# Hybrid decoder trunk on one core: the mixer's dense projections as numbered steps on TensorE, the small matmuls in runs between them

## Chip, cores and metric

One core of one Trainium2 chip. The metric is the device time of one execution in microseconds (us). The kernel computes in fp32; weights and activations of the large products are split into a rounded part (hi, type fp32r) and a remainder (lo), and the large products are hi·hi + hi·lo + lo·hi.

## The reference

The input x is 256 tokens x 2048. Each of two layers computes

```
h = rms_norm(x, mix_norm_w[l])
x = x + hybrid_mixer(h, w_in[l], ..., w_out[l])
h = rms_norm(x, ffn_norm_w[l])
x = x + (silu(h @ w_gate[l]) * (h @ w_up[l])) @ w_down[l]
```

and a last norm follows. `hybrid_mixer` takes one projection `h @ w_in` (7192 columns) apart into three groups of heads of 128: four mLSTM heads (mq, mk, mv, output gate mo), eight heads of forgetting attention, FoX (fq, fk, fv), and four gated DeltaNet heads (gq, gk, gv, output gate gz); 24 columns are gates. mLSTM and FoX are masked attention-like products over the 256 tokens with a decay from the gates; DeltaNet needs a triangular solve in chunks of 128. The heads' outputs are normed, gated, joined to y (256 x 2048) and multiplied by `w_out`.

## The kernel before

**Tiling.** Tokens are two tiles of 128. Weights come in units of at most 128 x 1024 (512 KB) through one DMA queue (SP's) into three buffers `raw`. For each unit ScalarE (ACT) rounds it to `whi` (L123) and VectorE (DVE) subtracts to get `wlo` (L124); both have four buffers, so unit n+4 can be rounded only when the matmuls that read unit n are done.

**Dense products.** `block_a` (L149 to 161) gives a transposed result, with the weights stationary: for a pair of 128-column outputs four units, first 32 matmuls of 512 columns on `whi` (L157), then 32 of 256 columns on `wlo` (L161). FoX's fq and fk, mLSTM's mq and mk, and DeltaNet's gkq and gvp are such pairs. `evac_a` (L163 to 170) empties one output of a pair: an ACT copy (L165), a DVE addition (L166), a DVE product (L168 or L170). `block_b` (L172 to 186) has the activations stationary and takes each unit's matmuls in threes (L184, L185, L186); mv, mog, mo, gz, fv and the output projection wo are of this kind. Their sums stand in four PSUM buffers (pool `pd`).

**Small products.** Everything between projections goes through the pool `pm`: two tags, `m` and `mg`, of two buffers each. `y_out` (L319 to 330) transposes one head's output with two matmuls against the identity (L323); an ACT and a DVE instruction (`split`, L205 and L206) empty it as hi and lo, the form in which wo wants it. The DeltaNet chain runs from the norms of q and k through the triangular solve (tiles lx, lt, lx2, lu2) and the state (y, s1p, o, ks, qs) to its last two scalings (L661, L662) and its transposes. FoX for one head is the scores fs, the maximum, two exponentials on ACT, three transposes fpt, a copy, and fo; after four heads come the sums' reciprocal, a power on POOL (L211) and a scaling of 128 x 1024 (L764), then the transposes.

**Order.** The kernel is written stage by stage: mv, mog, gates, mo, four pairs gkq, two pairs gvp, DeltaNet, gz, mLSTM heads, FoX in two groups of four heads, wo, then the feed-forward part. The framework's scheduler goes through the program with a model of the engines and may move an instruction ahead of others written earlier whenever its inputs are ready in the model; so a small product, written as one piece, ends up scattered in the dense matmuls that follow it. What comes out is one fixed queue for each engine, and each engine takes its queue strictly in order. Semaphores hold an instruction until the results that it reads are there, or until the buffer that it writes is free.

Of the kernel before, what the change touches and what calls it, by code (L numbers as in the profile page):

```python
# [12 lines left out]
F32 = mybir.dt.float32  # L13
F32R = mybir.dt.float32r
# [6 lines left out]
P = 128  # L21
# [38 lines left out]
def tile_trunk(ctx: ExitStack, tc: tile.TileContext, x: bass.AP, wu: bass.AP, prm: bass.AP,  # L60
               cst: bass.AP, fnw: bass.AP, out: bass.AP, depth: int, units: list):
    nc = tc.nc
    act, dve, pe, pool = nc.scalar, nc.vector, nc.tensor, nc.gpsimd
# [9 lines left out]
    pm = ctx.enter_context(tc.tile_pool(name="pm", bufs=2, space=bass.MemoryType.PSUM))  # L73
# [20 lines left out]
    def mps(name, tag="m"):  # L94
        return pm.tile([P, 512], F32, tag=tag, name=name)
# [235 lines left out]

    def mixer(l, norm, nxt):
        hs = norm.hs
        ys = [None] * KT

# [19 lines left out]


# [3 lines left out]
        pst = [dps("mog") for t in range(2)]  # L360
        block_b(l, "mog", 0, pst, hs, 0, KT, True, True, S + 24)
# [17 lines left out]
        ps = mps("gT")  # L379
        for t in range(2):  # L380
            pe.transpose(ps[:, t * P:(t + 1) * P], gtk[:, t], ident)
        act.copy(out=z, in_=ps[:, :S])
        gb = pr[:, l, R_GB:R_GB + 1]
        sgn = pr[:, l, R_SGN:R_SGN + 1]
        gcol = small("gcol", [3], 1)
        dve.tensor_scalar(out=gcol[:, 0:1], in0=gb, scalar1=1.0 / CAP, scalar2=None, op0=MUL)
        dve.tensor_tensor(out=gcol[:, 1:2], in0=gb, in1=sgn, op=MUL)
        dve.memset(gcol[0:32, 2:3], -1.0)
        act.activation(out=gcol[32:36, 2:3], in_=pr[32:36, l, R_AL:R_AL + 1], func=AF.Exp)
        dve.tensor_scalar(out=gcol[32:36, 2:3], in0=gcol[32:36, 2:3], scalar1=-1.0, scalar2=None, op0=MUL)  # L390
# [11 lines left out]
        dve.tensor_scalar(out=e[:36], in0=e[:36], scalar1=gcol[:36, 2:3], scalar2=None, op0=MUL)
        for c in range(2):
            sl = slice(c * P, (c + 1) * P)
            dve.tensor_tensor_scan(out=bl[:36, sl], data0=ones[:36].to_broadcast([36, P]), data1=e[:36, sl], initial=0.0, op0=MUL, op1=ADD)
        tot = bl[:12, P - 1:P]
        dve.tensor_scalar(out=br[:12, 0:P], in0=bl[:12, 0:P], scalar1=-1.0, scalar2=None, op0=MUL)
        dve.tensor_scalar(out=br[:12, P:2 * P], in0=bl[:12, 0:P], scalar1=-1.0, scalar2=tot, op0=MUL, op1=ADD)
        dve.tensor_scalar(out=br[:12, 2 * P:], in0=bl[:12, P:], scalar1=-1.0, scalar2=None, op0=MUL)

        r = rows[0:4]
        dve.scalar_tensor_tensor(out=r, in0=ti[0:4], scalar=CAP, in1=bl[0:4], op0=MUL, op1=SUB)
        mi1 = small("mi1", [1], 1)[0:4]
        dve.tensor_tensor_scan(out=mx[0:4, 0:P], data0=r[:, 0:P], data1=r[:, 0:P], initial=0.0, op0=MAX, op1=MAX)
        dve.tensor_tensor(out=mi1, in0=mx[0:4, P - 1:P], in1=bl[0:4, P - 1:P], op=ADD)
        dve.tensor_tensor_scan(out=mx[0:4, P:S], data0=r[:, P:], data1=r[:, P:], initial=mi1, op0=MAX, op1=MAX)
        dve.tensor_scalar(out=br[0:4, 0:P], in0=mx[0:4, 0:P], scalar1=-1.0, scalar2=None, op0=MUL)
        dve.tensor_scalar(out=br[0:4, P:2 * P], in0=mx[0:4, P:S], scalar1=-1.0, scalar2=bl[0:4, P - 1:P], op0=MUL, op1=ADD)
        dve.tensor_scalar(out=br[0:4, 2 * P:], in0=mx[0:4, P:S], scalar1=-1.0, scalar2=None, op0=MUL)
        dve.scalar_tensor_tensor(out=fl[0:4], in0=bl[0:4], scalar=-1.0, in1=mx[0:4, 0:S], op0=MUL, op1=SUB)  # L420
        act.copy(out=rows[64:68], in_=fl[0:4])
        act.copy(out=rows[32:36], in_=bl[32:36])
        bm = sp.tile([P, 384], BF16, tag="bm", name="bm", bufs=1)
        bg = sp.tile([P, S], BF16, tag="bg", name="bg", bufs=1)
        pool.memset(bm, 0.0)
        pool.memset(bg, 0.0)
        split3(bl[32:36], 4, 32, bg, (32, 0, 64), S, sd, gt4)
        split3(br[0:12], 12, 0, bm, (0, 32, 64), 384, sd, gt4)
        psc = mps("cols")
        for c in range(2):  # L430
            pe.transpose(psc[:, c * P:(c + 1) * P], rows[:, c * P:(c + 1) * P], ident)
        col = small("col", [2, 4, 4], 1)
# [21 lines left out]
        dt = g4("dt", [4, 2, P])
        for h in range(HG):
            ps = mps("dtp", "mg")
            row_bcast(ps[:, :S], h, bg, slice(0, S), True)
            for c in range(2):
                pe.matmul(ps[:, c * P:(c + 1) * P], identb, maskST, start=False, stop=(c == 1))
            for c in range(2):  # L460
                act.activation(out=dt[:, h, c], in_=ps[:, c * P:(c + 1) * P], func=AF.Exp, bias=ngc[:, c, h:h + 1])
# [21 lines left out]
        for h in range(HG):  # L483
            pss = [dps("gkq") for i in range(2)]
            block_a(l, [("in", off + h * P, ps) for off, ps in zip((O_GK, O_GQ), pss)], hs)
            conv_silu(pss[0], 4 + h, kT[:, h])
            conv_silu(pss[1], h, qT[:, h])
            ps = mps("qkt", "mg")
# [438 lines left out]
```

## Time and profile before

| | |
|---|---|
| Median of three runs | 2397.96 us (2397.83 to 2398.67) |
| Profiled execution, its own time | 2399.22 us |
| Its span, first to last instruction | 2397.4 us |
| PE busy | 2382.9 us, 99% of the span, 13344 instructions |
| PE's weight loads busy | 2081.5 us, 87% |
| DVE busy | 1477.3 us, 62%, 2246 instructions |
| ACT busy | 1194.7 us, 50%, 1879 instructions |
| POOL busy | 77.2 us, 3% |
| DMA | 436.11 MB, mean 182 GB/s |
| Mean granted TensorE clock | 0.999 of full speed |

PE is TensorE's matmuls, PEld its weight loads, SP the engine that issues the weight DMAs. Busy shares are means over the whole span; the waits view, the chain of waits and the timeline tell who waited for whom. Matmul records overlap one another, so the time that one of them takes in a stream is read from the chain of waits (its length over its count), not from its own duration.

### The profile page before, as it was taken

How to read it: one execution, taken by the hardware profiler on the slowest of the kernel's cores; microseconds unless marked ns; L12 is line 12 of the kernel's file. 1: busy time of each engine (PE TensorE's matmuls, PEld its weight loads, DVE VectorE, ACT ScalarE, POOL GpSimd, SP SyncE). 2: the span in 40 equal slices, each digit the busy share in tenths (PEclk: the TensorE clock that was granted, in tenths of full speed). 3: DMA queues.
4: the chain of work that ended last, by engine and by line, in shares of the span. 5: the costliest groups of instructions: out<-in, count | busy, mean ns of one | idle time of the engine just before them, and what ended most of it. 6: DMA issues, size and time to landing. Idle time of an engine off the chain costs nothing.

```text
span 2397.4 us, 34530 instructions
## 1 busy us (share of the span) xinstructions
PE 2382.9 (99%) x13344; PEld 2081.5 (87%) x13344; DVE 1477.3 (62%) x2246; ACT 1194.7 (50%) x1879; POOL 77.2 (3%) x107
## 2 busy tenths in 40 slices
PE   9999999999999999999999999999999999999998
PEld 8888888888888888888898888889888888888887
DVE  5896655566655655466558865565665556655665
ACT  6754554555434454444567545454544344544544
POOL 0220000000000000000003000000000000000000
PEclk9999999999999999999999999999999999999999
DMA  6554555465555656555655545454656555565564
GB/s 223 170 172 132 162 164 187 165 194 192 193 195 176 196 190 201 185 182 196 191 173 176 176 130 164 164 178 161 193 196 195 194 183 186 194 209 193 185 200 161
DMA packets 120885, 436.11 MB, mean 182 GB/s; under 512 B 13584, under 2 KB 14352, under 8 KB 120720
## 3 DMA queue, kind: packets, MB, share of 16 engines
q1 hardware_dynamic: 120160, 432.75, 55.6%
q8 instruction: 104, 1.70, 0.3%
q10 hardware_dynamic: 560, 1.15, 0.1%
q14 instruction: 61, 0.50, 0.1%
HBM read 431.76 MB, written 2.10 MB: 181 GB/s over the span
## 4 chain that ended last, share of the span: by engine, by line
PE 97%; ACT 1%; DVE 1%; DMA 1%; issue 0%; POOLq 0%; POOL 0%; DVEq 0%; ACTq 0%
PE pu L157 13%; PE pg L157 13%; PE pu L161 7%; PE pg L161 7%; PE dn L186 7%; PE dn L184 7%; PE dn L185 7%; PE wo L184 2%; PE wo L186 2%; PE wo L185 2%; PE fq L157 2%; PE fk L157 2%; PE gkq L157 2%; PE fk L161 1%; PE fq L161 1%; PE mk L157 1%
## 5 line engine op out<-in xcount | busy, mean ns | idle before, releaser
L124 DVE TENSOR_TENSOR wlo<-raw,whi 128x1024 fp32r<-128x1024 f32 (+2 forms) x821 | 990.6, 1217 | 654.7 <-ACT whi L123 429.3
L123 ACT ACTIVATE whi<-raw 128x1024 fp32r<-128x1024 f32 (+2 forms) x821 | 866.1, 1055 | 900.6 <-DMA raw<-wu 479.8
L157 PE MATMUL pu<-hl,whi 128*128 128x512 f32 x1408 | 350.2, 391 | 0.0
L157 PE MATMUL pg<-hl,whi 128*128 128x512 f32 x1408 | 336.9, 391 | 0.0
L157 PEld LDWEIGHTS pu<-hl,whi 128*128 128x128 f32 x1408 | 259.0, 188 | 50.3
L157 PEld LDWEIGHTS pg<-hl,whi 128*128 128x128 f32 x1408 | 259.0, 188 | 50.2
L185 PE MATMUL dn<-wlo,hid 128*128 128x512 f32 (+1 forms) x728 | 275.9, 379 | 0.0
L186 PE MATMUL dn<-whi,hid 128*128 128x512 f32 (+1 forms) x728 | 275.6, 379 | 0.0
L184 PE MATMUL dn<-whi,hid 128*128 128x512 f32 (+1 forms) x728 | 274.1, 379 | 0.0
L161 PEld LDWEIGHTS pg<-hl,wlo 128*128 128x128 f32 x1408 | 191.0, 190 | 13.1
L161 PE MATMUL pg<-hl,wlo 128*128 128x256 f32 x1408 | 195.1, 282 | 0.0
L161 PE MATMUL pu<-hl,wlo 128*128 128x256 f32 x1408 | 183.3, 283 | 0.0
L161 PEld LDWEIGHTS pu<-hl,wlo 128*128 128x128 f32 x1408 | 175.4, 192 | 0.2
L185 PEld LDWEIGHTS dn<-wlo,hid 128*128 128x128 f32 x728 | 137.0, 188 | 25.7
L186 PEld LDWEIGHTS dn<-whi,hid 128*128 128x128 f32 x728 | 136.9, 188 | 25.6
L184 PEld LDWEIGHTS dn<-whi,hid 128*128 128x128 f32 x728 | 136.6, 188 | 25.0
L184 PE MATMUL wo<-whi,yhl 128*128 128x512 f32 (+1 forms) x320 | 112.5, 353 | 0.0
L185 PE MATMUL wo<-wlo,yhl 128*128 128x512 f32 (+1 forms) x320 | 111.9, 350 | 0.0
L186 PE MATMUL wo<-whi,yhl 128*128 128x512 f32 (+1 forms) x320 | 111.0, 348 | 0.0
L820 DVE TENSOR_TENSOR hid<-up,hid 128x256 fp32r<-128x256 f32 x88 | 37.4, 424 | 90.5 <-ACT hid L819 90.5
L165 ACT COPY up<-pu 128x256 f32<-128x256 f32 x88 | 32.9, 373 | 111.5 <-PE pu L161 111.5
L157 PE MATMUL fk<-hl,whi 128*128 128x512 f32 x256 | 67.8, 401 | 0.0
(362 smaller groups left out, 2879.8 us busy)
## 6 DMA issues: line engine op xcount, KB each, us to landing
raw<-wu SPq DMA_DIRECT2D x808, 512.0 KB, 4.1
raw<-wu SPq DMA_DIRECT2D x10, 420.0 KB, 3.1
xall<-x SPq DMA_DIRECT2D x3, 512.0 KB, 8.3
fw<-fnw SPq DMA_DIRECT2D x2, 512.0 KB, 4.7
out<-xall ACTq DMA_DIRECT2D x2, 512.0 KB, 3.0
out<-xall SPq DMA_DIRECT2D x2, 512.0 KB, 3.0
xall<-x SPq DMA_DIRECT2D x2, 256.0 KB, 4.5
cst<-cst SPq DMA_DIRECT2D x1, 286.0 KB, 2.9
```

The costliest lines, as they stand in the source:

```text
L123: act.activation(out=whi[:, c], in_=raw[:, c], func=AF.Copy)
L124: dve.tensor_tensor(out=wlo[:, c], in0=raw[:, c], in1=f32(whi[:, c]), op=SUB)
L157: pe.matmul(ps, whi[:, i * P:(i + 1) * P], hs[half * 8 + i][2], start=(half + i == 0), stop=False)
L161: pe.matmul(ps[:, :S], los[2 * n + half][:, i * P:(i + 1) * P], hs[half * 8 + i][0], start=False, stop=(half == 1 and i == 7))
L165: act.copy(out=dst, in_=ps[:, S:])
L184: pe.matmul(pst[t][:, :w], hhi[:, sl], w1, start=st, stop=False)
L185: pe.matmul(pst[t][:, :w], hhi[:, sl], w2, start=False, stop=False)
L186: pe.matmul(pst[t][:, :w], hlo[:, sl], w1, start=False, stop=en)
L820: dve.tensor_tensor(out=lo, in0=up, in1=f32(hi), op=SUB)
```

## The change

The mixer's dense projections become steps in a fixed order on PE. `pe` is now an object that remembers its last instruction; `with pe.step()` tells the scheduler that everything in the block is issued after the last instruction of the step before. `dense_a` is one step (a whole `block_a`), `dense_b` two steps of eight k-tiles with a run between, one wo unit (two k-tiles) is a step. The chains of small products become generators: they stop at each `yield`, and `links()`, called between dense steps, is one step in which each living chain goes on to its next `yield`. Chains begun at the same time so advance in turn, and the small matmuls stand in runs between dense steps: 95 runs in place of 206 separate insertions, with the same 13032 matmuls of the same sizes. The start (mv), the wo tail and the feed-forward part are not in steps.

Three things go along. `pm` has one tag of four buffers in place of two tags of two. `y_out` takes a pair of heads: four transposes into one PSUM tile, emptied by two pairs of `split`. And mog's 16 k-tiles, cut in halves of eight, come as units of 3, 3, 2, 3, 3, 2 k-tiles in place of 3, 3, 3, 3, 3, 1.

```diff
+    class TensorE:
+        last, before = None, None
+        def matmul(self, *a, **k):
+            self.last = nc.tensor.matmul(*a, **k).ins
...
+        @contextmanager
+        def step(self):
+            with tc.issue_after(self.before) if self.before is not None else nullcontext():
+                yield
+            self.before = self.last
+        def free(self):
+            self.before = None
+    pe = TensorE()
...
-    pm = ctx.enter_context(tc.tile_pool(name="pm", bufs=2, space=bass.MemoryType.PSUM))
+    pm = ctx.enter_context(tc.tile_pool(name="pm", bufs=4, space=bass.MemoryType.PSUM))
...
-    def y_out(l, k, ytok, ys, tag="m"):
-        ps = mps("yT", tag)
-        for t in range(2):
-            pe.transpose(ps[:, t * P:(t + 1) * P], ytok(t), ident)
...
+    def y_out(l, k, ytok, ys):
+        ps = mps("yT")
+        for i in range(2):
+            for t in range(2):
+                pe.transpose(ps[:, i * S + t * P:i * S + (t + 1) * P], ytok(i, t), ident)
+        y = g4("yhl", [2, 2, S], F32R, "gy")
+        for i in range(2):
+            hi, lo = y[:, 0, i], y[:, 1, i]
+            split(ps[:, i * S:(i + 1) * S], pr[:, l, R_YW + k + i:R_YW + k + i + 1], hi, lo)
+            ys[k + i] = (hi, lo)
...
+        def links():
+            with pe.step():
+                for chain in list(chains):
+                    if next(chain, StopIteration) is StopIteration:
+                        chains.remove(chain)
+        def start(chain):
+            next(chain)
+            chains.append(chain)
...
+        def dense_b(mat, col, name, w=512):
+            pst = [dps(name + str(t)) for t in range(2)]
+            for i in range(2):
+                if i:
+                    links()
+                with pe.step():
+                    block_b(l, mat, col, pst, hs[i * 8:], i * 8, 8, i == 0, i == 1, w)
+            return pst
+        def dense_a(cols):
+            with pe.step():
+                block_a(l, cols, hs)
...
+            yield
+            ps = heads(lambda h: (an[:, 1, h], ug[:, h]), "o1")
+            dve.tensor_tensor(out=og[:, 1], in0=ps, in1=tg, op=ADD)
...
+            dve.tensor_tensor(out=ogf, in0=ogf, in1=ag.unsqueeze(2).to_broadcast([P, 8, P]), op=MUL)
+            dve.tensor_tensor(out=ogf, in0=ogf, in1=gt.rearrange("p t (h x) -> p (t h) x", h=4), op=MUL)
+            yield
+            for h in range(0, HG, 2):
+                y_out(l, 12 + h, lambda i, t: og[:, t, h + i], ys)
...
+        for g in range(2):
+            fv = evac_b(dense_b("in", O_FV + g * 512, "fv"), "fv")
+            fo = g4("fo", [2, 4, P], tag="gd")
+            rs = small("rs", [2, 2, 4])
+            links()
             for hh in range(4):
-                y_out(l, 4 + g * 4 + hh, lambda t: fo[:, t, hh], ys, "mg" if hh % 2 else "m")
+                h = g * 4 + hh
+                qk = qk_of(("fq", "fk"), O_FQ + h * P, O_FK + h * P, ISD, None)
+                links()
+                start(fox(g, hh, qk, fv, fo, rs))
...
             for i, k in enumerate(ks):
-                block_b(l, "out", n * 512, pst, ys[k:k + 2], k, 2, first and i == 0, last and i == len(ks) - 1)
+                with pe.step():
+                    block_b(l, "out", n * 512, pst, ys[k:k + 2], k, 2, first and i == 0, last and i == len(ks) - 1)
+                if chains and i % 2:
+                    links()
```

A FoX chain yields ahead of fs, ahead of fpt, ahead of fo and (the fourth head of a group) ahead of the transposes; the DeltaNet chain yields 18 times, the first when it is started.

What this does to the queues is shown at two places, the same in both layers; the rows are layer 0's.

**DeltaNet's last transposes.** On PE before, in the FoX part (yT are the transposes of DeltaNet's output `at`, L323; L157 and L161 are dense):

```order
L157 MATMUL fq<-hl,whi 128x512 x15
L157 MATMUL fk<-hl,whi 128x512 x8
L161 MATMUL fq<-hl,wlo 128x256 x4
L157 MATMUL fk<-hl,whi 128x512
L323 MATMUL yT<-ident,at 128x128 x4
L157 MATMUL fk<-hl,whi 128x512 x7
L161 MATMUL fq<-hl,wlo 128x256 x12
```

and now (every matmul has the line of the wrapper, L70, every transpose L73):

```order
L70 MATMUL o_3327<-xx,dt 128x128 x4
L70 MATMUL fo<-fv,fp_3228 128x128 x3
L70 MATMUL fq<-hl,whi 128x512 x16
L70 MATMUL fk<-hl,whi 128x512 x16
L70 MATMUL fq<-hl,wlo 128x256 x16
L70 MATMUL fk<-hl,wlo 128x256 x16
L73 MATMUL yT<-ident,at 128x128 x8
L73 MATMUL yT<-ident,fo 128x128 x8
L70 LDWEIGHTS cb
L70 MATMUL fs<-bm,cb 128x128
```

One whole dense step now lies between DeltaNet's last product o and its transposes, which stand with FoX's transposes and the next head's fs in one run of five `pm` tiles. On DVE before, up to the scalings that the transposes read (L661, L662; `ag` is the scale that L655 makes from the norm `ro`):

```order
L210 TENSOR_SCALAR ro_1780<-so_1758 128x8
L124 TENSOR_TENSOR wlo_2679<-raw_2676,whi_2678 128x1024
L655 SCALAR_TENSOR_TENSOR ag_1776<-ro_1780,rqs_1775 128x8
L661 TENSOR_TENSOR at_1283<-at_1283,ag_1776 128x1024
L662 TENSOR_TENSOR at_1283<-at_1283,gt_1933 128x1024
L124 TENSOR_TENSOR wlo_2693<-raw_2690,whi_2692 128x1024
```

and now (the scalings are L718 and L719, wlo is L145, the evacuation of fq and fk L187, L189, L191, the hi-lo split of a transposed output L227):

```order
L231 TENSOR_SCALAR ro_3354<-so_3333 128x8
L145 TENSOR_TENSOR wlo_3535<-raw_3532,whi_3534 128x1024
L716 SCALAR_TENSOR_TENSOR ag_1257<-ro_3354,rqs_3350 128x8
L145 TENSOR_TENSOR wlo_3549<-raw_3546,whi_3548 128x1024
L187 TENSOR_TENSOR fqkT_3379<-fq_3380,fqkT_3379 128x256
L718 TENSOR_TENSOR at_1594<-at_1594,ag_1257 128x1024
L145 TENSOR_TENSOR wlo_3563<-raw_3560,whi_3562 128x1024
L191 SCALAR_TENSOR_TENSOR fqkT_3379<-fqkT_3379,rb_367 128x256
L187 TENSOR_TENSOR fqkT_3379<-fk_3381,fqkT_3379 128x256
L719 TENSOR_TENSOR at_1594<-at_1594,gt_1706 128x1024
L145 TENSOR_TENSOR wlo_3577<-raw_3574,whi_3576 128x1024
L189 TENSOR_TENSOR fqkT_3379<-fqkT_3379,rb_367 128x256
```

L718 and L719 now stand behind the evacuation of fq and fk of the dense step that PE runs before the transposes; wlo_3535, 3549, 3563 and 3577 are the four units of the step after the transposes.

**FoX's last transposes, in wo.** On DVE before (L764 is the scaling of the second FoX group, L762 makes its factor):

```order
L210 TENSOR_SCALAR rf_3833<-fva_3830 128x8
L124 TENSOR_TENSOR wlo_4047<-raw_4044,whi_4046 128x1024
L762 TENSOR_TENSOR rf_3833<-rf_3833,finv_3828 128x8
L764 TENSOR_TENSOR fo_3326<-fo_3326,rf_3833 128x1024
L124 TENSOR_TENSOR wlo_4065<-raw_4062,whi_4064 128x1024
```

and now (L852 and L854 are the same two):

```order
L231 TENSOR_SCALAR rf_3937<-fva_3934 128x8
L145 TENSOR_TENSOR wlo_4039<-raw_4036,whi_4038 128x1024
L852 TENSOR_TENSOR rf_3937<-rf_3937,finv_3932 128x8
L854 TENSOR_TENSOR fo_3201<-fo_3201,rf_3937 128x1024
L145 TENSOR_TENSOR wlo_4057<-raw_4054,whi_4056 128x1024
```

DVE's order is the same here; what moved is PE: the transposes of this scaling now stand two wo steps (24 matmuls of 512 columns) behind the last fo. The last of the matmuls that free the buffer for whi_4038 and wlo_4039 is that of the first of these two steps.

## Rows read from the trace of the kernel before

**Rows 1.** The page, busy time by engine, and the chain that ended last by engine.
```profile
PE 2382.9 (99%) x13344; PEld 2081.5 (87%) x13344; DVE 1477.3 (62%) x2246; ACT 1194.7 (50%) x1879; POOL 77.2 (3%) x107
...
PE 97%; ACT 1%; DVE 1%; DMA 1%; issue 0%; POOLq 0%; POOL 0%; DVEq 0%; ACTq 0%
```

**Rows 2.** PE's waits by releaser: us in total, times, longest.
```profile
PE xT L245 <- DMA xall<-x: 4.7, 1, 4.7
...
PE cols L431 <- ACT gt L421: 0.6, 1, 0.6
PE dtp L443 <- DVE bg L317: 0.4, 1, 0.4
```

**Rows 3.** Stretches of layer 0: length, then busy time of each engine in it.
```profile
20.00:122.00 102.00, 101.02 (x636) 90.93 (x635) 72.37 (x122) 69.25 (x143) 17.50 (x29) 1.00 0.56 179
...
338.80:470.00 131.20, 131.20 (x763) 115.45 (x762) 75.45 (x103) 67.92 (x121) 2.06 (x2) 1.00 0.54 177
```

**Rows 4.** Chain of waits from 250 to 256 us: start, us, what.
```profile
250.19 1.81 PE fk L157 x8
...
254.77 1.31 PE fq L161 x11
```

**Rows 5.** Chain of waits from 64.5 to 72 us, up to the gates' transposes.
```profile
64.71 1.15 DVE wlo L124
...
69.06 0.41 PE cols L431 x2
```

**Rows 6.** Chain of waits from 198 to 206 us, round a 64-row group.
```profile
199.63 0.60 PE lx L613 x8
200.24 1.27 PE mk L161 x9
```

**Rows 7.** Chain of waits from 1500 to 1503 us, round single transposes.
```profile
1501.64 0.11 PE fpt L744
1501.75 0.23 PE fv L184
```

**Rows 8.** Timeline from 243.5 to 256 us: DeltaNet's last scaling and transposes.
```profile
247.19 1.23 DVE L662 TENSOR_TENSOR at<-at,gt 128x1024 f32<-128x1024 f32 x1
...
252.54 0.60 PE L323 MATMUL yT<-ident,at 128*128 128x128 f32 x4
```

**Rows 9.** VectorE by line and shape, 200 to 470 us: count, busy, mean ns, idle before.
```profile
L124 DVE TENSOR_TENSOR wlo<-raw,whi 128x1024 fp32r<-128x1024 f32 x87 | 105.7, 1221 | 55.4 <-ACT whi L123 48.0 <-ACT fo L752 3.6 <-issue 1.8
L206 DVE SCALAR_TENSOR_TENSOR yhl<-yT,pr,yhl 128x256 fp32r<-128x256 f32 x16 | 6.8, 477 | 12.6 <-ACT yhl L205 12.6
...
L166 DVE TENSOR_TENSOR fqkT<-fk,fqkT 128x256 f32<-128x256 f32 x8 | 3.3, 414 | 0.0
...
L662 DVE TENSOR_TENSOR at<-at,gt 128x1024 f32<-128x1024 f32 x1 | 1.2, 1226 | 0.0
```

**Rows 10.** ScalarE by line and shape, 200 to 470 us.
```profile
L123 ACT ACTIVATE whi<-raw 128x1024 fp32r<-128x1024 f32 x85 | 90.0, 1060 | 90.6 <-DMA raw<-wu 33.7 <-PE wo L186 33.6 <-PE fv L186 10.9
L205 ACT ACTIVATE yhl<-yT,pr 128x256 fp32r<-128x256 f32 x16 | 6.3, 469 | 0.9 <-PE yT L323 0.9
...
L165 ACT COPY fqkT<-fk 128x256 f32<-128x256 f32 x8 | 3.0, 374 | 9.6 <-PE fk L161 9.6
```

**Rows 11.** Timeline from 1578 to 1596 us: the last FoX scaling of layer 1.
```profile
1585.32 1.06 ACT L123 ACTIVATE whi<-raw 128x1024 fp32r<-128x1024 f32 x1
...
1587.76 0.17 DVE L762 TENSOR_TENSOR rf<-rf,finv 128x8 f32<-128x8 f32 x1
...
1587.96 1.23 DVE L764 TENSOR_TENSOR fo<-fo,rf 128x1024 f32<-128x1024 f32 x1
...
1593.74 1.03 PE L323 MATMUL yT<-ident,fo 128*128 128x128 f32 x8
```

**Rows 12.** Chain of waits from 5 to 14 us, the first matmuls.
```profile
8.08 0.85 PE xT L245 x4
...
12.89 0.44 PE xT L245 x4
```

More of the change, by code (lines that the diff above doesn't have):

```diff
@@ L1 @@
-from contextlib import ExitStack
+from contextlib import ExitStack, contextmanager, nullcontext
 import numpy as np
@@ L92, in dps, with mps @@
         return pd.tile([P, 512], F32, tag="d", name=name)
-    def mps(name, tag="m"):
-        return pm.tile([P, 512], F32, tag=tag, name=name)
+    def mps(name):
+        return pm.tile([P, 512], F32, tag="m", name=name)
     def f32(ap):
@@ L334, in mixer @@
         ys = [None] * KT
+        chains = []
+        def links():
[6 more added lines that the diff above has]
+            chains.append(chain)
         def evac_b(pst, name):
@@ L354, in mixer @@
                            scale=rstd[:, t:t + 1])
+        pe.free()
         mo = g4("mo", [2, 512], tag="gd")
@@ L359, in mixer @@
         pool.memset(gtk, 0.0)
-        pst = [dps("mog") for t in range(2)]
-        block_b(l, "mog", 0, pst, hs, 0, KT, True, True, S + 24)
+        pst = dense_b("mog", 0, "mog", S + 24)
         for t in range(2):
@@ L402, in mixer @@
[L402 to L422, printed above, removed]
+        gcol = small("gcol", [3], 1)
@@ L423, in mixer @@
         bm = sp.tile([P, 384], BF16, tag="bm", name="bm", bufs=1)
         bg = sp.tile([P, S], BF16, tag="bg", name="bg", bufs=1)
[L425 to L432, printed above, removed]
@@ L448, in mixer @@
+        start(gates())
+        pst = dense_b("in", O_MO + S, "mo", S)
         for t in range(2):
@@ L451, in mixer @@
         dve.tensor_scalar(out=mo, in0=mo, scalar1=0.5, scalar2=0.5, op0=MUL, op1=ADD)
[L454 to L461, printed above, removed]
+        links()
         def conv_silu(ps, blk, dst):
@@ L482, in mixer, with norms @@
         ke, s1 = kes1[:, 0], kes1[:, 1]
[L483 to L488, printed above, removed]
+        def norms(h):
+            yield
+            ps = mps("qkt")
             for i, src in enumerate((kT, qT)):
@@ L526, in mixer @@
+        for h in range(HG):
+            pss = [dps("gkq") for i in range(2)]
+            dense_a([("in", off + h * P, ps) for off, ps in zip((O_GK, O_GQ), pss)])
+            conv_silu(pss[0], 4 + h, kT[:, h])
+            conv_silu(pss[1], h, qT[:, h])
+            links()
+            start(norms(h))
+        start(deltanet(small("ag", [8], 1)))
         for h in range(0, HG, 2):
             pss = [dps("gvp") for i in range(2)]
-            block_a(l, [("in", O_GV + (h + i) * P, pss[i]) for i in range(2)], hs)
+            dense_a([("in", O_GV + (h + i) * P, pss[i]) for i in range(2)])
@@ L529, in mixer @@
             for i in range(2):
                 conv_silu(pss[i], 8 + h + i, vT[:, h + i])
-        for h in range(HG):
-            ps = mps("vt", "mg")
-            for c in range(2):
-                pe.transpose(ps[:, c * P:(c + 1) * P], vT[:, h, c * P:(c + 1) * P], ident)
-            for c in range(2):
-                act.activation(out=zz[:, c, h], in_=ps[:, c * P:(c + 1) * P], func=AF.Copy, scale=nk[:, c, h:h + 1])
-        tt, tn, xx = g4("tt", [2, 4, P]), g4("tn", [1024]), g4("xx", [2, 4, P])
@@ L572, in heads @@
-        def heads(fn, name):
-            ps = mps(name, "mg")
-            for h in range(4):
-                lhsT, rhs = fn(h)
-                pe.matmul(ps[:, h * P:(h + 1) * P], lhsT, rhs, start=True, stop=True)
-            return ps.rearrange("p (h x) -> p h x", h=4)
-        def spread(src):
-            for q in QUADS:
-                dve.transpose(out=ttf[q, :, q], in_=src[q])
-        def level(m, t, x, b):
-            for lhs, rhs, dst in ((m, t, x), (ttf, x, None)):
-                ps = mps("lx" if dst is not None else "lt", "mg")
-                for n in range(8):
-                    pe.matmul(ps[:, n * b:(n + 1) * b], lhs[:, n], rhs[:, n], start=True, stop=True)
-                ps = ps[:, :8 * b].rearrange("p (n x) -> p n x", n=8)
-                if dst is not None:
-                    act.copy(out=dst, in_=ps)
-            return ps
@@ L604, in mixer @@
-        act.activation(out=t64[:, :, 32:64], in_=t32, func=AF.Copy, scale=par(3))
-        for q in (0, 2):
-            dve.transpose(out=ttf[QUADS[q], :, QUADS[q + 1]], in_=t64[QUADS[q + 1], :, 0:32])
-        for c in range(2):
-            ps = mps("lx2", "mg")
-            lo, hi = slice(0, 64), slice(64, P)
-            x2s = tn[:, 0:512].rearrange("p (c h x) -> p c h x", c=2, h=4)
-            for h in range(4):
-                pe.matmul(ps[hi, h * 64:(h + 1) * 64], at[lo, c, h, hi], t64[lo, c * 4 + h], start=True, stop=True)
-            x2 = x2s[hi, c]
-            dve.tensor_scalar(out=x2, in0=ps[hi, 0:S].rearrange("p (h x) -> p h x", h=4), scalar1=-1.0, scalar2=None,
-                              op0=MUL)
-            ps = mps("lu2", "mg")
-            for h in range(4):
-                pe.matmul(ps[lo, h * 64:(h + 1) * 64], x2s[hi, c, h], tt[hi, c, h, hi], start=True, stop=True)
-            act.copy(out=tt[lo, c, :, hi], in_=ps[lo, 0:S].rearrange("p (h x) -> p h x", h=4))
@@ L622, in mixer @@
-        og = at
-        ug, tg = xx[:, 0], xx[:, 1]
-        def colb(ap):
-            return ap.unsqueeze(2).to_broadcast([P, 4, P])
-        ps = heads(lambda h: (tt[:, 0, h], zz[:, 0, h]), "y0")
-        dve.tensor_tensor(out=ug, in0=ps, in1=colb(br1[:, 0]), op=MUL)
-        ps = heads(lambda h: (ke[:, h], ug[:, h]), "s1p")
-        act.copy(out=s1, in_=ps)
-        ps = heads(lambda h: (an[:, 0, h], ug[:, h]), "o0")
-        act.copy(out=og[:, 0], in_=ps)
-        ps = heads(lambda h: (kT[:, h, P:], s1[:, h]), "ks")
@@ L643, in mixer @@
-        so = small("so", [8], 1)
-        for c in range(2):
-            for h in range(HG):
-                junk = sp.tile([P, P], BF16, tag="junkg", name="junkg", bufs=1)
-                act.activation(out=junk, in_=og[:, c, h], func=AF.Square, accum_out=so[:, c * 4 + h:c * 4 + h + 1])
-        rqs = small("rqs", [8], 1)
-        ag = small("ag", [8], 1)
-        dve.tensor_scalar(out=rqs, in0=rq.rearrange("p a b -> p (a b)"), scalar1=0.5 * ISD, scalar2=None, op0=MUL)
-        dve.tensor_tensor(out=so, in0=so, in1=rqs, op=MUL)
@@ new lines, in mlstm @@
+            if h < HM - 1:
+                return
+            den = small("den", [2, 4], 1)
+            for i in range(2):
+                dv = mn[i][:, :, :, P:P + 1].rearrange("p t h o -> p t (h o)")
+                dve.scalar_tensor_tensor(out=den[:, :, 2 * i:2 * i + 2], in0=dv, scalar=-1.0, in1=dv, op0=MUL, op1=MAX)
+            dve.tensor_tensor(out=den, in0=den, in1=ef, op=MAX)
+            inv = small("inv", [2, 4], 1)
+            dve.reciprocal(out=inv, in_=den)
+            mva = small("mva", [2, 4], 1)
@@ new lines, in mlstm @@
+            dve.tensor_tensor(out=mva, in0=mst[:, :, :, 1:2].rearrange("p t h o -> p t (h o)"), in1=inv, op=MUL)
+            dve.tensor_tensor(out=mva, in0=mva, in1=inv, op=MUL)
+            rm = rstd_of(mva.rearrange("p t h -> p (t h)"), 1, "rm", 8).rearrange("p (t h) -> p t h", t=2)
+            dve.tensor_tensor(out=rm, in0=rm, in1=inv, op=MUL)
+            for h in range(HM):
+                for t in range(2):
+                    num = mn[h // 2][:, t, h % 2, 0:P]
+                    dve.tensor_scalar(out=num, in0=num, scalar1=mst[:, t, h, 0:1], scalar2=rm[:, t, h:h + 1], op0=SUB,
+                                      op1=MUL)
+                    dve.tensor_tensor(out=mo[:, t, h * P:(h + 1) * P], in0=num, in1=mo[:, t, h * P:(h + 1) * P], op=MUL)
@@ new lines, in mlstm, with qk_of @@
+            yield
+            for h in range(0, HM, 2):
+                y_out(l, h, lambda i, t: mo[:, t, (h + i) * P:(h + i + 1) * P], ys)
+        def qk_of(names, cq, ck, sq, sk):
+            qk = sp.tile([P, 2, S], F32, tag="qk", name=names[0] + "kT", bufs=2)
+            pq, pk = dps(names[0]), dps(names[1])
+            dense_a((("in", cq, pq), ("in", ck, pk)))
+            evac_a(pq, qk[:, 0], rb, sq)
+            evac_a(pk, qk[:, 1], rb, sk)
+            return qk
+        for h in range(HM):
+            qk = qk_of(("mq", "mk"), O_MQ + h * P, O_MK + h * P, None, ISD)
+            links()
+            start(mlstm(h, qk))
@@ new lines, in fox @@
+        def fox(g, hh, qk, fv, fo, rs):
+            h = g * 4 + hh
+            yield
+            ps = mps("fs")
+            row_bcast(ps[:, :P], 4 + h, bm, slice(0, P), True)
+            pe.matmul(ps[:, :P], identb, maskQK, start=False, stop=False)
+            pe.matmul(ps[:, :P], qk[:, 0, :P], qk[:, 1, :P], start=False, stop=True)
+            row_bcast(ps[:, P:384], 4 + h, bm, slice(P, 384), True)
+            pe.matmul(ps[:, S:384], identb, maskQK, start=False, stop=False)
+            pe.matmul(ps[:, P:384], qk[:, 0, P:], qk[:, 1], start=False, stop=True)
+            nm = small("nm", [2])
+            dve.tensor_reduce(out=nm[:, 0:1], in_=ps[:, :P], axis=AX.X, op=MAX, negate=True)
+            dve.tensor_reduce(out=nm[:, 1:2], in_=ps[:, P:384], axis=AX.X, op=MAX, negate=True)
+            pt = sp.tile([P, 384], F32, tag="pt", name="fp", bufs=2)
+            act.activation(out=pt[:, :P], in_=ps[:, :P], func=AF.Exp, bias=nm[:, 0:1], accum_out=rs[:, 0, 0, hh:hh + 1])
+            act.activation(out=pt[:, P:], in_=ps[:, P:384], func=AF.Exp, bias=nm[:, 1:2],
+                           accum_out=rs[:, 0, 1, hh:hh + 1])
+            yield
+            ps = mps("fpt")
+            for i in range(3):
+                pe.transpose(ps[:, i * P:(i + 1) * P], pt[:, i * P:(i + 1) * P], ident)
+            p2 = sp.tile([P, 384], F32, tag="p2", name="fp2", bufs=2)
+            dve.tensor_copy(out=p2, in_=ps[:, :384])
+            yield
+            ps = mps("fo")
+            vs = slice(hh * P, (hh + 1) * P)
+            pe.matmul(ps[:, :P], p2[:, :P], fv[:, 0, vs], start=True, stop=True)
+            pe.matmul(ps[:, P:S], p2[:, P:S], fv[:, 0, vs], start=True, stop=False)
+            pe.matmul(ps[:, P:S], p2[:, S:], fv[:, 1, vs], start=False, stop=True)
+            act.copy(out=fo[:, :, hh], in_=ps[:, :S].rearrange("p (t x) -> p t x", t=2))
+            for t in range(2):
+                junk = sp.tile([P, 512], BF16, tag="junk", name="junk", bufs=1)
+                act.activation(out=junk[:, :P], in_=fo[:, t, hh], func=AF.Square, accum_out=rs[:, 1, t, hh:hh + 1])
+            if hh < 3:
+                return
@@ L778, in mixer @@
             wout(n, pst, early, True, False)
+        assert not chains
+        pe.free()
         for n in range(2):
```

411 lines of the change are left out of this document (231 added, 180 removed).

## The prediction

> **What bounds the kernel now.** I read the page first, for the bound: PE is busy 99% of the span, and the chain that ended last is 97% PE; DVE, with 62%, and ACT are far from it [rows 1]. Busy shares can hide idle time, so PE's waits come next: behind the start, with 4.7 us for the first piece of x, only two are listed, 0.6 us for `cols` and 0.4 us for `dtp`, both once, in the gates [rows 2]. The stretches of layer 0 say the same: from 20 to 122 us PE works 101.02 of 102.00 us, from 338.8 to 470 us all of 131.20 [rows 3]. So the mixer is one unbroken stream of matmuls, and the scheduler's scattering of small products costs no waiting. That decides the question: a new order of the same matmuls can gain the 1.0 us of waits and what the hand-overs between dense and small cost, and it can lose any time by which a run comes before its inputs are ready.
>
> **What a dense step gives as cover.** A matmul of 512 columns takes 1.81 / 8 = 0.226 us, one of 256 columns 1.31 / 11 = 0.119 [rows 4]. A dense step of a pair is 32 x 0.226 + 32 x 0.119 = 11.0 us; a wo step is 12 x 0.226 = 2.7 us. A chain whose answer takes longer than the steps between two runs stops PE, since PE has nothing else in its queue.
>
> **Gains.**
> 1. *Hand-overs.* 206 insertions become 95, 111 fewer. A single transpose between two dense matmuls takes 0.11, the next dense 0.23 [rows 7]: against 0.226 that is at most 0.01 to 0.02 each, so 111 of them are worth 0 to 2.2 us. Groups of 64 rows cost more: after one (0.60 us for eight), nine matmuls of 256 columns take 1.27 in place of 9 x 0.119 = 1.07, so 0.2 us is lost behind it [rows 6], and some 0.1 ahead of it by my estimate from eight times 0.06. Each layer has four such pieces in three insertions, and two runs after: 0.3 x 2 = 0.6 us. I take -1.5 (ends -0.6 and -2.8).
> 2. *The two gate waits.* `cols` comes at 69.06, at the end of a chain of DVE and ACT work in which a wlo of 1.15 us stands [rows 5]. After the change `cols` stands behind half of mo and a whole gkq step, 5.7 + 11.0 us behind the gates' transposes, and `dtp` another step later. I take it that both waits go: -1.0 (ends 0 and -1.0).
> 3. *One yT tile for two heads, a common `pm`.* The same transposes and the same split instructions: nothing. mog's units: as many DMAs, bytes and matmuls: nothing, and the DMA share of these stretches is 0.54 to 0.56 [rows 3]. POOL's few instructions move with their chains; its queue is busy 3% [rows 1].
>
> **Costs.** All come from DVE or ACT finishing after the dense step that should cover them.
>
> 4. *DeltaNet's transposes, twice.* In DVE's new queue L719, which yT reads, stands behind the evacuation of fk, and fk's last matmul is the last of the dense step. Before, the same scaling ended at 247.19 + 1.23 = 248.4, and its transposes came at 252.5 [rows 8]: 4.1 us to spare. Now, with the run ahead of the step as zero: seven small matmuls, 0.8; the dense step until 11.8. ACT copies fk (0.374 [rows 10]), DVE adds (0.414) and L719 takes 1.23 [rows 9]: PE waits at least 2.0 us, whatever else happens. But DVE isn't free at 11.8. wlo_3535 and wlo_3549 need the buffers of the dense step's own wlo, free after 8 and 16 of its 256-column matmuls, at 0.8 + 7.2 + 1.0 = 9.0 and 9.9. From 9.0 DVE's queue runs: wlo 1.22, `ag` about 0.17, wlo 1.22, fq's addition 0.41, L718 1.23, wlo 1.22, fq's product 0.41, fk's addition 0.41, L719 1.23 [rows 9]. That is 7.5 us, 7.7 with 0.03 between two, so it ends at 16.7, and PE waits 4.9. If wlo_3535 gets through earlier, the queue from 9.9 on gives 16.2 and 4.4. I take 4.7 each (ends 2.0 and 5.2).
> 5. *fs behind these transposes, twice.* The run takes five `pm` tiles of four buffers. fs needs the first yT tile emptied. Sixteen transposes take 16 x 0.11 = 1.8 us. DVE, from L719 on, has wlo 1.22, 0.41, then three splits of 0.477 [rows 9] before that tile is free: 3.1 us, so 1.4 more (ends 0.3, if DVE has the wlo behind it, and 1.6). The Trainium skill, "Perfetto Trace Analysis", section "Matmuls", says that independent groups should rotate through PSUM banks so that emptying one overlaps the next group's matmuls. By that rule alone a rotation of four hides the emptying and this term is nothing; the sum would be 2.8 us lower. The rows speak against it: four transposes take 0.44 [rows 12], emptying what they made takes two ACT and two DVE instructions of 0.47 each [rows 9, 10].
> 6. *FoX's transposes in wo, twice.* Two wo steps (5.4 us) lie between the last fo and yT. whi_4038 gets its buffer when the first step ends, 2.7 us before. Then come whi 1.06, wlo 1.22, L852 0.17 and L854 1.23, in a row [rows 11, 9]: 3.7 us with nothing between, 3.8 with gaps. PE waits 1.0 to 1.1; before, yT came at 1593.74, 4.5 us after L764's end [rows 11]. I take 1.0 (ends 0 and 1.3).
> 7. *qkt behind four dtp tiles, twice:* the fifth tile again. ACT's two exponentials of 128 columns on the first dtp run while PE issues the other three; the nearest row is a 256-column copy, 0.374 [rows 10]. I take 0.1 (ends 0 and 0.3).
>
> All other runs I set against the step that covers them: the nearest is fs next to DeltaNet's s1p and o products in one run, where the time needed and the cover come out equal; nothing there.
>
> **Sum.** 2 x (4.7 + 1.4 + 1.0 + 0.1) - 1.5 - 1.0 = +11.9 us. On the profiled execution's 2399.2 that is 2411.1; the median of the runs shown is 1.3 lower, so I expect 2410. All costs at their low and gains at their high end: 2 x 2.3 - 3.8 = +0.8; the other way round 2 x 8.4 - 0.6 = +16.2.
>
> **Rivals.**
> - *Not slower: the runs are ready in time.* Place: L719. If its inputs let DVE finish it within the dense step, only the gains of 2.5 us and smaller waits remain. It decides at 2.0 us: the wait of item 4 must go altogether, which means that L719 is done ahead of fk's evacuation. The idle DVE speaks for it (over a third of its time [rows 1]); against it that its queue is fixed, and that L719 stands in it behind an instruction that needs the step's last matmul. With items 5 to 7 at their low ends, 2 x 0.3, that gives 2396; as taken, 2 x 2.5, 2400. I give it 0.15.
> - *The clock falls in the wait.* At the start, after PE had stood idle for 4.7 us, four transposes take 0.85 us, and from 12.89 on 0.44 [rows 2, 12]: half speed at first, 1.2 of 2.4 GHz by the spacing, for at most the 8.2 us from 4.7 to 12.9. Half of that, 4.1 us, is the most that was lost. If a wait of 4.7 us within the stream does the same, I take 3 us for each as an estimate, and there are two: +6, 2416. Against it: the only long idle time in the trace lies ahead of all work, and shows no fall, only a late rise. The Trainium skill, "TensorE: Matmul & The Clock Gate", section "HAM oscillation — how this bites in real kernels", describes such a fall in the midst of a kernel where PE waits for DMA; no stretch of this trace shows one. I give 0.1.
> - *The order isn't as written.* If the scheduler still scattered, nothing would change: 2398. The queues show the runs, so 0.04.
>
> **Numbers.** The forecast has 0.67, the clock 0.10, runs in time 0.15, no real change 0.04, something else 0.04. This measurement can tell some 0.2%, 4.8 us, from no change. The forecast and the clock are beyond it: slower 0.77. Runs in time and no real change lie within it: same 0.19. Faster by 4.8 us is more than all gains together at their high ends (3.8), so it needs something that I don't see: 0.04. The range runs from 2400 (items 4 to 6 near their low ends) to 2417 (the high ends, or the clock on top of the forecast).
>
> **What would show it.** In the profile after, PE's waits list yT <- DVE with the longest about 4.7 us, twice, fs <- DVE about 1.4 and yT <- fo about 1.0, and `cols` and `dtp` are gone; the timeline has L719 ending about 4.7 us behind fk's last matmul. The dense steps keep 0.226 and 0.119. It would be wrong if yT shows no wait, if a wait stands at another tile, or if dense matmuls after a wait take 0.43 (the clock).

## The result, and the profile after

| | before | after |
|---|---|---|
| Median | 2397.92 us | 2414.07 us (2413.22 to 2418.45) |
| Ratio | | 1.007, 95% interval 1.0053 to 1.0088 |
| Profiled execution, its span | 2399.22, 2397.4 us | 2414.18, 2412.4 us |

The change costs 16.1 us, 15.0 between the two profiled executions. The page gives PE 3.2 us more busy time, so most of the loss is idle time or work that leaves gaps:

```profile
PE 2386.1 (99%) x13344; PEld 2087.8 (87%) x13344; DVE 1476.4 (61%) x2246; ACT 1191.1 (49%) x1879; POOL 76.7 (3%) x107
```

PE's waits by releaser (us in total, times, longest) answer to [rows 2]:

```profile
PE yT L73 <- DVE at L719: 8.2, 2, 4.1
PE xT L73 <- DMA xall<-x: 4.1, 1, 4.1
PE qkt L73 <- ACT dt L502: 3.1, 2, 2.7
PE yT L73 <- DVE fo L854: 2.2, 2, 1.1
PE mv L70 <- ACT whi L144: 1.1, 1, 1.1
```

`cols` and `dtp` are gone from the list, and three new waits stand there. The largest is DeltaNet's transposes. Its place in the timeline (start, us, engine, line, what; the bracket is the idle time before it):

```profile
338.15 1.23 DVE L145 TENSOR_TENSOR wlo<-raw,whi 128x1024 fp32r<-128x1024 f32 x1 [0.57 <-PE fq L70]
...
339.42 1.22 DVE L145 TENSOR_TENSOR wlo<-raw,whi 128x1024 fp32r<-128x1024 f32 x1
...
340.56 0.42 DVE L187 TENSOR_TENSOR fqkT<-fq,fqkT 128x256 f32<-128x256 f32 x1
340.89 1.22 DVE L718 TENSOR_TENSOR at<-at,ag 128x1024 f32<-128x1024 f32 x1
341.03 0.37 ACT L186 COPY fqkT<-fk 128x256 f32<-128x256 f32 x1 [1.54 <-PE fk L70]
342.02 1.22 DVE L145 TENSOR_TENSOR wlo<-raw,whi 128x1024 fp32r<-128x1024 f32 x1
...
343.16 0.42 DVE L191 SCALAR_TENSOR_TENSOR fqkT<-fqkT,rb 128x256 f32<-128x256 f32 x1
343.49 0.42 DVE L187 TENSOR_TENSOR fqkT<-fk,fqkT 128x256 f32<-128x256 f32 x1
343.83 1.22 DVE L719 TENSOR_TENSOR at<-at,gt 128x1024 f32<-128x1024 f32 x1
...
345.10 1.97 PE L73 MATMUL yT<-ident,at 128*128 128x128 f32 x8 [4.11 <-DVE at L719]
```

PE's dense step is over at 341.0. DVE is then busy without a gap until 345.05, in just the order that its queue has, and PE starts right behind L719.

What follows is seen in the windows of PE (stretch, length, busy time of each engine with its count, granted clock, DMA share, GB/s):

```profile
335.00:341.00 6.00, 5.99 (x42) 5.44 (x40) 4.43 (x10) 2.40 (x5) 1.76 (x3) 1.00 0.13 40
345.10:349.80 4.70, 4.70 (x25) 4.45 (x26) 4.08 (x9) 2.91 (x8) 0.00 (x0) 0.66 0.60 209
349.80:354.00 4.20, 4.20 (x20) 3.42 (x19) 1.24 (x4) 2.88 (x7) 0.00 (x0) 1.00 0.00 0
1280.90:1284.00 3.10, 3.10 (x11) 2.53 (x10) 2.85 (x6) 3.10 (x10) 2.14 (x2) 0.57 0.77 251
402.20:405.00 2.80, 2.77 (x17) 2.46 (x18) 2.66 (x5) 1.83 (x5) 0.00 (x0) 1.00 0.61 227
```

The granted clock was 1.00 before the wait, 0.66 on average in the 4.7 us behind it, and 1.00 again after that: between its two levels, 1.2 and 2.4 GHz, so mostly the lower one. Behind qkt's wait in layer 1 it was 0.57, and five matmuls of 512 columns there stood 0.43 us apart by their ends, against 0.226 in [rows 4]. Behind the wait in wo, of 1.1 us, it stayed at 1.00. The chain of waits has the price behind yT's wait: the 16 transposes of this run take 3.52 us, 0.22 each, against 0.11 in [rows 12].

```profile
343.91 1.14 DVE at L719
345.06 0.04 issue
345.10 3.52 PE yT L73 x16
348.62 1.15 PE fs L70 x8
349.77 3.68 PE fq L70 x16
```

**Where the 15.0 us come from.** I took the time from the end of each matmul to the end of the next, less what the same pair takes inside a stream. So measured, a wait is a little longer than in the waits view, since restarting counts too.

| term | us |
|---|---|
| yT behind L719, 4.47 and 4.43 | +8.9 |
| slow matmuls behind it, 1.6 and 2.2 | +3.8 |
| qkt behind the dtp tiles, 0.61 and 3.04 | +3.6 |
| slow matmuls behind the second of these | +1.3 |
| FoX's yT in wo, 1.31 twice | +2.6 |
| `cols` and `dtp` of before, 0.79, 0.54, 0.34 | -1.7 |
| start: x came 0.6 earlier, the ten mv behind it took 0.6 less | -1.2 |
| left over, put down to fewer hand-overs | -2.3 |
| sum | 15.0 |

The start differs from profile to profile: the first xT comes at 4.1 to 4.8 us in the eight of this case, and the ten mv take 3.96 us in [rows 12] (8.93 to 12.89) and 3.32 here:

```profile
8.35 3.32 PE mv L70 x10
```

The profiled execution of the kernel before was 1.3 us over its median, that of the changed kernel 0.1, so the medians differ by about 1 us more than the profiles do.

### The profile page after: what moved, and what is told of

The parts are those of the page before. It is cut to its first block, busy times and chain, and to the rows that moved or that the text cites. A ratio compares the mean times of both kernels' runs of the same rounds, so it can differ in the third digit from the quotient of the medians.

```text
span 2412.4 us, 34538 instructions
## 1 busy us (share of the span) xinstructions
PE 2386.1 (99%) x13344; PEld 2087.8 (87%) x13344; DVE 1476.4 (61%) x2246; ACT 1191.1 (49%) x1879; POOL 76.7 (3%) x107
## 4 chain that ended last, share of the span: by engine, by line
PE 97%; DVE 1%; DMA 1%; ACT 1%; issue 0%; POOLq 0%; POOL 0%; DVEq 0%; ACTq 0%; SPq 0%
PE pu L70 20%; PE pg L70 20%; PE dn L70 20%; PE wo L70 7%; PE fq L70 4%; PE fv L70 4%; PE fk L70 4%; PE gkq L70 2%; PE mv L70 2%; PE gvp L70 2%; PE mq L70 2%; PE mk L70 2%; PE gz L70 2%; PE mog L70 1%; PE mo L70 1%; PE fs L70 1%
## 5 line engine op out<-in xcount | busy, mean ns | idle before, releaser
L145 DVE TENSOR_TENSOR wlo<-raw,whi 128x1024 fp32r<-128x1024 f32 (+2 forms) x821 | 989.9, 1217 | 753.0 <-ACT whi L144 464.4
L70 PE MATMUL dn<-whi,hid 128*128 128x512 f32 (+1 forms) x1504 | 440.7, 376 | 0.0
L70 PE MATMUL pu<-hl,whi 128*128 128x512 f32 x1408 | 350.2, 391 | 0.0
L70 PE MATMUL pg<-hl,whi 128*128 128x512 f32 x1408 | 336.9, 391 | 0.0
L70 PEld LDWEIGHTS dn<-whi,hid 128*128 128x128 f32 x1504 | 276.1, 188 | 50.8
L70 PEld LDWEIGHTS pu<-hl,whi 128*128 128x128 f32 x1408 | 259.0, 188 | 50.4
L70 PEld LDWEIGHTS pg<-hl,whi 128*128 128x128 f32 x1408 | 259.0, 188 | 50.3
L70 PE MATMUL dn<-wlo,hid 128*128 128x512 f32 (+1 forms) x752 | 282.6, 376 | 0.0
L70 PEld LDWEIGHTS pg<-hl,wlo 128*128 128x128 f32 x1408 | 191.0, 190 | 13.1
L70 PE MATMUL pg<-hl,wlo 128*128 128x256 f32 x1408 | 195.1, 282 | 0.0
L70 PE MATMUL pu<-hl,wlo 128*128 128x256 f32 x1408 | 183.3, 283 | 0.0
L70 PEld LDWEIGHTS pu<-hl,wlo 128*128 128x128 f32 x1408 | 175.4, 192 | 0.2
L70 PE MATMUL wo<-whi,yhl 128*128 128x512 f32 (+1 forms) x640 | 169.8, 351 | 0.0
L70 PEld LDWEIGHTS dn<-wlo,hid 128*128 128x128 f32 x752 | 141.5, 188 | 25.6
L70 PEld LDWEIGHTS wo<-whi,yhl 128*128 128x128 f32 x640 | 112.5, 189 | 14.7
L70 PE MATMUL wo<-wlo,yhl 128*128 128x512 f32 (+1 forms) x320 | 111.4, 348 | 0.0
L70 PE MATMUL fv<-whi,hl 128*128 128x512 f32 x256 | 81.4, 394 | 0.0
L70 PEld LDWEIGHTS wo<-wlo,yhl 128*128 128x128 f32 x320 | 60.6, 189 | 7.3
L70 PE MATMUL fq<-hl,whi 128*128 128x512 f32 x256 | 63.5, 400 | 0.0
```

The lines of the kernel that those rows point to most:

```text
L70: self.last = nc.tensor.matmul(*a, **k).ins
L145: dve.tensor_tensor(out=wlo[:, c], in0=raw[:, c], in1=f32(whi[:, c]), op=SUB)
```

## The experiments

All medians are compared with 2397.9 to 2398.3 us of the kernel before, timed beside them, and with the 2414.07 above.

**e1_dn_later: DeltaNet's transposes one dense step later.**

```diff
+            yield
             yield
             for h in range(0, HG, 2):
                 y_out(l, 12 + h, lambda i, t: og[:, t, h + i], ys)
```

> The changed kernel with one more yield ahead of DeltaNet's transposes, so that they stand one dense step (11.0 us) later. Theory A (they stand too close behind L719, and the wait lets the clock fall): both waits of 4.5 us go and with them the slow transposes and fs behind them, 1.6 and 2.2 us: 2414.1 - 8.9 - 3.8 = about 2401.4, no granted clock under 1 in the FoX part. Theory B (the slow matmuls have another cause than the wait): only the 8.9 us go, 2405, and the clock still falls there. Theory C (DVE is so far behind that the next run waits instead): 2411 to 2414.

Measured: 2401.8 us (2399.69 to 2404.63 in 10 runs), ratio to before 1.0016 (1.0007 to 1.0025). Its waits in the mixer and a window over the same place:

```profile
...
PE qkt L73 <- ACT dt L502: 3.8, 2, 3.2
PE yT L73 <- DVE fo L855: 2.2, 2, 1.1
...
```
```profile
340.00:360.00 20.00, 20.00 (x127) 17.92 (x126) 17.37 (x30) 11.83 (x24) 0.00 (x0) 1.00 0.57 184
```

Theory A: one bare `yield` gives back 12.3 of the 16.1 us, the wait at yT and the low clock behind it go together, and nothing waits in its place. Both went at once here; e5 takes them apart.

**e2_dtp_2and2: the dtp tiles in two runs.**

```diff
             for h in range(HG):
+                if h == 2:
+                    yield
                 ps = mps("dtp")
```

> The changed kernel with the four dtp tiles in two runs of two, so that qkt is the third tile of its run. Theory A (qkt waits for the buffer of the first dtp, whose exponentials stand in ACT's queue behind a weight that came late): the waits of 0.4 and 2.7 us and the slow stretch of 1.3 us behind the second go, 5.0 us by the ends of the matmuls: about 2409. Theory B (the late weight stops PE anyway, at the next dense step): the first layer gains 0.5 us, the second only part, 2412 to 2413.5.

Measured: 2409.48 us (2408.97 to 2409.88), ratio 1.0047 (1.0035 to 1.006): 4.6 us less, theory A. qkt is out of the list of waits:

```profile
PE yT L73 <- DVE at L721: 8.1, 2, 4.1
PE xT L73 <- DMA xall<-x: 4.8, 1, 4.8
PE yT L73 <- DVE fo L856: 2.2, 2, 1.1
PE mv L70 <- ACT whi L144: 1.1, 1, 1.1
```

**e6_dtp_later: the four tiles together, one dense step later.** Why qkt waited 0.4 us in layer 0 and 2.7 in layer 1 is in the timeline of the changed kernel, layer 1:

```profile
1278.20 1.06 ACT L144 ACTIVATE whi<-raw 128x1024 fp32r<-128x1024 f32 x1 [2.31 <-DMA raw<-wu]
1279.16 0.63 ACT L186 COPY xc<-gkq 128x256 f32<-128x256 f32 x2
...
1279.68 2.19 ACT L502 ACTIVATE dt<-dtp,ngc 128x128 f32<-128x128 f32 x8
...
1280.37 0.69 PE L73 MATMUL qkt<-ident,gk 128*128 128x128 f32 x2 [2.68 <-ACT dt L502]
```

The exponentials that empty the first dtp tile stand in ACT's queue behind the whi of a later weight, and ACT sat 2.31 us waiting for that weight to land.

```diff
             yield
+            yield
             for h in range(HG):
                 ps = mps("dtp")
```

> The changed kernel with the four dtp tiles in one run still, but one dense step later, away from the gate work on DVE. Theory A (qkt's wait is small by itself and grows where a weight comes late in front of the exponentials on ACT): 0.4 us in both layers, no slow stretch behind: 2414.1 - 2.4 - 1.3 = about 2410.5. Theory B (the fifth tile alone costs it): again 0.4 and 2.7 us, 2414.

Measured: 2411.61 us (2409.92 to 2412.52), 2.5 less; forecast by theory A were 3.6. The wait is small now:

```profile
PE qkt L73 <- ACT dt L503: 0.5, 1, 0.5
```

By the ends of the matmuls it is 0.35 and 0.68 us, and the clock stays up behind it. In the new place ACT waits only 0.7 us for the weight ahead of the exponentials, in place of 2.31. So the fifth tile with a weight that comes nearly in time costs about half a microsecond, and the rest goes with the late weight ahead of it on ACT. In this kernel fs also waits 0.3 us once, which takes back a little.

**e3_fox_later: FoX's last transposes four wo steps behind the last fo.**

```diff
             yield
+            if g:
+                yield
             for hh in range(0, 4, 2):
                 y_out(l, 4 + g * 4 + hh, lambda i, t: fo[:, t, hh + i], ys)
```

> The changed kernel with one more yield ahead of the second FoX group's transposes, which then stand four wo steps behind the last fo, not two. Theory A (two wo steps are too short for whi, wlo and the scaling): both waits of 1.1 us (1.3 by the ends of the matmuls) go, about 2411.5. Theory B (DVE has no room in wo): a wait of the same size at the late wo units or the next transposes, 2414.

Measured: 2413.39 us (2411.01 to 2414.76). The waits in wo are gone, and no other stands in wo:

```profile
PE yT L73 <- DVE at L719: 8.1, 2, 4.1
PE xT L73 <- DMA xall<-x: 4.3, 1, 4.3
PE qkt L73 <- ACT dt L502: 3.5, 2, 2.6
PE mv L70 <- ACT whi L144: 1.1, 1, 1.1
PE fs L70 <- DVE yhl L227: 0.3, 1, 0.3
```

The median fell by 0.7 us only, within the scatter of 3.8 us; by time alone this run is inconclusive. The trace decides for theory A, and the next run has the time. This trace shows one thing more: qkt waited 2.6 us in layer 1, nearly as long as in the changed kernel, and behind this wait the clock did not fall:

```profile
1280.60:1284.00 3.40, 3.40 (x18) 2.87 (x18) 3.15 (x6) 3.40 (x13) 1.86 (x2) 1.00 0.69 223
```

**e4_all_three: e1, e2 and e3 together.**

> All three edits together. If they add up, 2414.1 - 12.7 - 5.0 - 2.6 = about 2393.8, no wait of PE left in the mixer: 4 us under the kernel before (2397.9), of which 1.7 are its two gate waits and some 2.4 its hand-overs. If the runs with fewer hand-overs gain nothing, 2396 to 2398. If waits move elsewhere, over 2398.

Measured: 2394.78 us (2394.15 to 2395.54 in 11 runs), ratio to before 0.9987 (0.9978 to 0.9996). It is faster than both kernels: 3.1 us under the one before. The edits add up, to within 1.0 us of the 2393.8 expected, and the mixer has no wait left; these two lines are the whole list, and two stretches of layer 0 that answer to [rows 3] are full:

```profile
PE xT L73 <- DMA xall<-x: 4.7, 1, 4.7
PE mv L70 <- ACT whi L144: 1.1, 1, 1.1
```
```profile
20.00:122.00 102.00, 102.00 (x635) 92.10 (x634) 74.50 (x125) 69.72 (x144) 19.30 (x30) 1.00 0.57 187
338.80:470.00 131.20, 131.20 (x767) 115.81 (x766) 80.95 (x115) 70.10 (x130) 3.01 (x4) 1.00 0.51 175
```

Its span is 2393.0 us, 4.4 under that of before. x comes at the same time, but the ten first mv are 0.6 us shorter:

```profile
8.99 3.38 PE mv L70 x10
```

So some 0.5 of the 4.4 us are the start and 1.7 the gate waits; 2.2 remain for the hand-overs. By the medians, 3.1 us apart, 1.4 remain.

**e5_fill: matmuls in place of the wait.**

```diff
         ps = mps("yT")
+        for _ in range(20 if fill else 0):
+            pe.matmul(ps, fill[0][0][:, :P], fill[1][2], start=True, stop=True)
```

`fill` is the list of normed activations for DeltaNet's first pair of heads, nothing for the others.

> The changed kernel with 20 extra matmuls of 512 columns (4.5 us at full speed), whose result is overwritten, on PE ahead of DeltaNet's transposes in each layer: PE works where it waited. They write the first yT tile. Theory A (the idle time lets the clock fall; the slow transposes then gave DVE time to empty the tiles, which hid fs's wait): no wait or one under 0.5 us at yT, transposes 0.11 us each, and fs now waits about 1.4 us for the fifth buffer: 2414.1 - 3.8 + 2.8 = about 2413. Theory B (transposes in a run are slow for another reason): they still take 0.22 each, and the time is 2414 or more.

Measured: 2411.52 us (2410.93 to 2412.46). The chain of waits of layer 1, the new wait, and a window of layer 0 behind its wait:

```profile
1540.11 4.56 PE yT L70 x20
1544.67 0.45 PE yT L73 x4
...
1545.65 1.76 DVE yhl L227 x4
1547.41 0.05 issue
1547.46 1.22 PE fs L70 x8
```
```profile
PE fs L70 <- DVE yhl L227: 2.8, 2, 1.8
```
```profile
350.30:354.00 3.70, 3.70 (x20) 3.15 (x21) 2.02 (x6) 2.35 (x7) 0.00 (x0) 1.00 0.15 60
```

Theory A: with PE at work the transposes take 0.11 us each, and now fs waits for the fifth buffer, 1.8 and 1.0 us, 2.8 together. In the changed kernel the slow transposes had hidden such a wait. In layer 0 of e5 a weight that came late, for which ACT waited 3.4 us, stands ahead of the splits on DVE, so its 1.8 us are more than the fifth tile alone costs. The time is 1.5 us under the forecast of 2413; qkt's waits were 2.0 us in this profile in place of 3.1, and the clock stayed at 1.00 behind them.

## Why the prediction was right

Forecast +11.9 us, 2410 (2400 to 2417); measured +16.1, 2414.07. The sign held, and so did the largest term with its mechanism: yT's wait, 8.9 of the 15.0 us. That the total lies in the range is in part luck, since terms that came out dearer and terms that came out cheaper partly cancelled. By its items:

- **1, hand-overs**, -1.5 (-0.6 to -2.8): -2.3 as the rest of the account, -2.2 in e4 by the profiles and -1.4 by its medians. In the range; whether it was taken too small stays open.
- **2, gate waits**, -1.0: both went. By the ends of the matmuls they were worth 1.7, since the waits view leaves out the restart and a small one of layer 1.
- **4, DeltaNet's transposes**, 4.7 each: 4.47 and 4.43. DVE's queue ran in the order worked out, wlo_3549 from 339.42, L719 to 345.05. From wlo_3535 at 338.15 that is 6.9 us where 7.7 were added up: each instruction starts some 0.08 us before the record of the one ahead ends, and the sum had put 0.03 between them. That takes 0.8 off the 4.9 us and leaves the 4.1 of the waits view. The bound without the queue was 2.0, so reading the order of the queue was worth more than half of this term. e1 shows that the wait hangs on this one place.
- **5, fs on the fifth buffer**, 1.4 each: this term did not come: nothing in the changed kernel, 1.8 and 1.0 in e5. The wait was worked out with transposes of 0.11 us; at 0.22 they give DVE the time it needs. The chain of e5 also has four splits ahead of fs where three were counted. By the rule of the Trainium skill, "Perfetto Trace Analysis", section "Matmuls", the rotation hides the emptying; where PE ran at full speed (e5) it did not.
- **6, FoX's transposes in wo**, 1.0 each: 1.1 in the waits view, 1.31 by the ends.
- **7, qkt**, 0.1 each (0 to 0.3): this step failed. It measured 0.61 and 3.04 us, with 1.3 of slow matmuls behind the second. I had priced the exponentials from the moment when their tile is ready, and not looked at what stands ahead of them in ACT's queue: two copies and the whi of a weight that was late. e2 and e6 show it.
- **The clock** stood as a rival with a chance of 0.1 and 3 us for each fall, six in all. It came, with 1.6 and 2.2 us behind yT and 1.3 behind qkt, 5.1 together. [Rows 12] had the halved speed only at the start; the windows after show it in the midst of the kernel. Its sign was one of those that the forecast had named for being wrong, dense matmuls of 0.43 us after a wait, and it showed. The Trainium skill, "TensorE: Matmul & The Clock Gate", section "HAM oscillation — how this bites in real kernels", describes such falls where PE waits for DMA; the trace has them with DVE (4.1 us) and ACT (2.7 us) as what PE waited for.

So the total came out some 4 us short, out of larger errors of both signs: between the profiles 9.1 us upward (wo, qkt, clock) and 6.0 downward. Between the profiled executions: 11.9 - 0.5 (yT) - 2.8 (fs) + 0.6 (wo) + 3.4 (qkt) + 5.1 (clock) - 0.7 (gates) - 0.8 (hand-overs) - 1.2 (start) = 15.0. What was not tried: which of the pieces in front of L719 on DVE would have to go for yT's wait to vanish without another step, and the common `pm`, the paired yT tile and mog's units each by itself; e4 shows only that with them and no waits the kernel is not slower than before.

## What to carry to other kernels

When a scheduler's free order is replaced by a fixed one on the engine that bounds, each run is a deadline: go through the queues of the engines that feed it, in their new order, and count everything that stands ahead of the producer, evacuations of the covering step itself above all. Three kinds of runs, each placed too early, cost more here than 111 fewer insertions gained, and three `yield`s turned the loss into a gain. And where a wait leaves the bounding engine idle, look at the granted clock behind it before you add up.

## What the runs showed of the hardware

- After waits of 4.1 and 2.7 us of PE the granted clock fell (0.66 and 0.57 in the stretches behind them); after waits of 1.8 us (e5) and 1.1 us it stayed at 1.00, and so it did after one of 2.6 us in e3. What decides at such lengths stays open. A fall cost 1.3 to 2.2 us.
- The slower clock can hide another wait: fs's waits, 2.8 us in e5, where PE was kept at work, are absent from the changed kernel and 0.3 us in e3 and e6.
- Most kernels in which qkt waits behind the late weight scatter more: 4.9 us between runs in e1, 5.2 in the changed kernel, 3.8 in e3, against 0.9 in e2 and 1.4 in e4, where this wait is gone. e5, which has the wait, scatters by 1.5 in four runs, and the kernel before, which hasn't, by 2.3 in 21; that the wait is the cause is not shown.
